# A hybrid encoder trunk in float32: where waiting work stands in VectorE's and ScalarE's order, how early the output projections load, and where the residual's factor goes

## The chip, the cores and the metric

The kernel runs on one core of a Trainium2 chip. The metric is the device time of one execution in microseconds (us), from the first to the last instruction with what lies around it; lower is better. The times shown are the median of three runs. The trace is one further execution that the hardware profiler recorded.

## The reference, cut to what matters

Two layers over a sequence of 2048 tokens of width 1024, in float32. Layer 0 mixes windowed attention with a gated short convolution, layer 1 mixes multi-head latent attention (8 heads, full 2048 x 2048 scores) with chunked spatial gating. Both end alike:

```python
def odd_mixer(x, pos, w_in, ...):
    cq, ckv, kr, du, dv, z = _split(x @ w_in, ODD_SIZES)
    ...
    yc = mla_attention(q_nope, q_rope, k_nope, k_rope, v)       # softmax(q k^T * scale) v, per head
    yd = chunked_spatial_gate(jax.nn.gelu(du), jax.nn.gelu(dv), v_ln_g, v_ln_b, w_s, b_s)
    y = jnp.concatenate([rms_norm(yc, c_norm), rms_norm(yd, d_norm)], axis=-1) * jax.nn.silu(z)
    return y @ w_out

# per layer i:
    h = layer_norm(DEEPNORM_ALPHA * x + y, post_ln_g[i], post_ln_b[i])      # ALPHA = 4 ** 0.25
    x = h + jax.nn.sigmoid(h @ ple_gate[i]) * (p[i] @ ple_proj[i])
```

Every matrix product is done to nearly full float32 accuracy: an operand is split into a rounded high part (`ScalarE` copy) and the low rest (a subtraction on `VectorE` or `GpSimd`), and a product takes three matmuls (high x high, high x low, low x high).

## The kernel before

There are four stages: `phase_a` (input projection of layer 0 with its mixers), `phase_out(0)` (its output projection and what follows it), `phase_c` (input projection of layer 1, spatial gating, latents, queries and keys), and `phase_d` (latent attention), which at its end starts `phase_out(1)`.

**Order of the work.** The program is traced in Python; a planner then chooses each engine's order from its own simulated times, and may move an instruction ahead of others on its engine when it thinks that the inputs are there. Each engine, and SP, which issues nearly all DMAs, then works strictly in that order. In `phase_d` TensorE alone keeps the order as traced. `tc.issue_after(ins)` (used by the change) makes what a block traces on the engine of `ins` stand behind `ins` in that engine's order.

**Attention (`phase_d`).** 8 heads x 4 query chunks of 512 are 32 blocks; a block goes over 16 key tiles (`kb`) of 128. Per key tile: three score matmuls (L1246 to 1248), the exponential on ScalarE in place in PSUM (L1249), the split into `ph` (ScalarE) and `pl` (VectorE, both L66/67 by way of L1252), the addition of `ph` into `acc` on GpSimd (L1257, L1259), one matmul for the row maxima of the block after next and its reduction on VectorE (L1136, L1137), and the two value matmuls (L1186, L1187) four key tiles later (`LAG`). `ph` has 7 buffers, `pl` 6, the scores 4 PSUM tiles. While block b runs, block b-1 is finished: at `kb` 3 its outputs leave for DRAM, at `kb` 7 its `acc` is split, at `kb` 9 `reciprocals` sums it over partitions with two matmuls, writes that row to DRAM, reads it back as 128 x 4 together with the sums of the low parts, adds (L1218), takes the reciprocal (L1219) and writes `rec` to DRAM. At the start of blocks 6, 9, ..., 27 one weight tile of the next stage is loaded and split (`out_weight`, L524). Operands of head h+1 are loaded in the blocks around its first use, through SP.

**Output projection (`phase_out`).** 16 token blocks of 128 tokens. `load(t)` (L572) loads the residual into `ox` and scales it by the square root of 2 on ScalarE (L576), and loads the operand tiles `ou` (three buffers, two per token block). In layer 1 the attention half of `ou` is made here from the three parts of the attention output: added on GpSimd (L594), times the broadcast `rec` (L595), squared for the RMS norm (L596), times the gate, split; `yc` and `szt` have one buffer, `ycm` and `rec` come from a ring of three raw tiles that the weight loads and the gate's input `praw` share. `first(t)` (L607) does the projection (48 matmuls), the scaled addition to the residual (L618) and the layer norm; `second(t)` (L628) transposes, multiplies by the two gate matrices (60 matmuls), and writes the result. The loop runs `first(t + 1)`, then `second(t)`. For layer 1, `next(self.output)` in the last attention block (L1269) loads the last two weight tiles and token block 0.

Of the kernel before, what the change touches and what calls it, by code (L numbers as in the profile page):

```python
# [31 lines left out]
SUM_AT = 9  # L32
START_AT = 2
# [19 lines left out]
class Builder:  # L53
# [467 lines left out]
    def out_weights(self, rings, src, ks, after=None):  # L521
        return list(self.out_weight(rings, src, ks, after))

    def out_weight(self, rings, src, ks, after=None):  # L524


        for k in ks:
# [6 lines left out]
            self.dma(raw, src[k * P:(k + 1) * P])  # L534
            eng = self.nc.gpsimd if k % 2 and src.shape[0] == D else self.nc.vector
# [18 lines left out]
    def phase_out(self, layer, es=None, wo=None, w_out=None, w_pr=None, right=None):  # L554


        tc, nc, I, c, d = self.tc, self.nc, self.i, self.c, self.d
# [9 lines left out]
        if right:  # L567
            w_out = w_out + self.out_weights(wo, I["w_out"][layer], range(len(w_out), 8))
            lng, lnb = self.out_norm(of, layer)
        xs, us = {}, {}  # L570

        def load(t):  # L572
            ts = slice(t * P, (t + 1) * P)
            x = xs[t] = xr.tile([P, D], F32, name="ox")
            self.dma(x, xin[ts])
            nc.scalar.activation(x, x, AF.Copy, scale=math.sqrt(2.0))  # L576
            us[t] = []
            for h in range(2):
                u = of.tile([P, 2, 4, P], F32R, name="ou", tag="ou", bufs=3)
                us[t].append(u)  # L580
                if layer == 1 and h == 0:
                    yc = of.tile([P, 4, P], F32, name="yc", tag="yc", bufs=1)
                    self.dma(yc, d["yc"][0, :, :, ts])
                    more = self.rr.tile([P, 2, 4, P], F32, name="ycm")
                    for a in range(2):
                        self.dma(more[:, a], d["yc"][1 + a, :, :, ts])
                    rec = self.rr.tile([P, 4, P], F32, name="rec")
                    for a in range(2):
                        self.dma(rec[64 * a:64 * a + 64],
                                 d["rec"].rearrange("(k a) s -> a k s", a=2)[a][:, ts].partition_broadcast(64))  # L590
                    sz = of.tile([P, 4, P], F32, name="szt", tag="szt", bufs=1)
                    self.dma(sz, d["szc"][:, :, ts])
                    for a in range(2):
                        nc.gpsimd.tensor_tensor(yc, yc, more[:, a], ALU.add)  # L594
                    nc.vector.tensor_tensor(yc, yc, rec, ALU.mult)  # L595
                    nc.scalar.activation(rec, yc, AF.Square)  # L596
                    nc.vector.tensor_tensor(sz, yc, sz, ALU.mult)
                    nc.gpsimd.tensor_tensor(rec[:, 0:2], rec[:, 0:2], rec[:, 2:4], ALU.add)
                    nc.gpsimd.tensor_tensor(rec[:, 0], rec[:, 0], rec[:, 1], ALU.add)
                    self.colsum(ss[:, 0, t:t + 1], rec[:, 0], self.psC("cs"))  # L600
                    self.rms(rs, ss, 0, slice(t, t + 1))
                    self.split(u[:, 0], u[:, 1], sz)
                    continue
                for a in range(2):
                    self.dma(u[:, a], d[ud][:, a, 4 * h:4 * h + 4, ts])

        def first(t):  # L607
            if t not in xs:
                load(t)
# [81 lines left out]
        for t in range(NB):  # L691
            if t + 1 < NB:
                first(t + 1)
            second(t)
# [688 lines left out]
```

## Time and profile before

| | us |
|---|---|
| median of three runs | 2961.62 (2958.94 to 2961.75) |
| the profiled execution's own time | 2963.46 |
| its span, first to last instruction | 2961.7 |
| TensorE busy | 2848.6 (96%) |
| VectorE busy | 1980.3 (67%) |
| ScalarE busy | 1351.7 (46%) |
| GpSimd busy | 1091.9 (37%) |

By the first and last instructions of each stage's lines, `phase_a` takes the first 720 us, `phase_out(0)` the next 430, `phase_c` up to 1683, attention from 1682.7 to 2493.8, `phase_out(1)` the rest. In the profile PE is TensorE, DVE VectorE, ACT ScalarE, POOL GpSimd, SP the queue that issues DMAs. A busy TensorE may still run at half its clock. A number in square brackets behind an instruction is the time its engine stood idle before it, with what ended that.

### The profile page before, as it was taken

Reading aid. Unit: us, or ns where it says so; the run is one execution under the profiler, and the core shown is the slowest. Engines: PE = TensorE matmul, PEld = TensorE weight load, DVE = VectorE, ACT = ScalarE, POOL = GpSimd, SP = SyncE. Lnnn points to the kernel's source line nnn. Section 1 sums busy time; section 2 is a strip of 40 time slices with the busy share of each in tenths; the row PEclk is TensorE's granted clock in tenths of the full one; section 3 lists DMA queues with packets and bytes.
Section 4 is the critical chain, followed back from the end, with each engine's and each line's share of the span. In section 5 each row is a group of like instructions: output and inputs, shape, how many; then the busy total and the mean of one; then the engine's idle time right before and its main releaser. Section 6 shows DMA issues by size and latency. Waiting matters only on the chain.

```text
span 2961.7 us, 38334 instructions
## 1 busy us (share of the span) xinstructions
PE 2848.6 (96%) x12808; PEld 2311.6 (78%) x12808; DVE 1980.3 (67%) x3956; ACT 1351.7 (46%) x2507; POOL 1091.9 (37%) x832
## 2 busy tenths in 40 slices
PE   8999999999999999999999999999999997799999
PEld 7888888888788888888888777777677765677787
DVE  3788467886644455446756788888888875456665
ACT  3554345454211123233432488888788875111111
POOL 0011001112411110120103187888888887423331
PEclk9999999999999999999999999999999998899999
DMA  7654465445444447216773403331333133333341
GB/s 227 181 144 138 142 192 161 131 125 191 137 119 132 127 132 265 85 62 231 247 236 93 114 17 81 81 81 25 81 84 70 48 81 90 101 106 114 106 116 43
DMA packets 316599, 365.27 MB, mean 123 GB/s; under 512 B 33248, under 2 KB 244368, under 8 KB 311280
## 3 DMA queue, kind: packets, MB, share of 16 engines
q1 hardware_dynamic: 288752, 333.38, 38.9%
q10 hardware_dynamic: 27648, 29.43, 2.8%
q8 instruction: 101, 1.65, 0.2%
q14 instruction: 98, 0.80, 0.1%
HBM read 238.19 MB, written 124.53 MB: 122 GB/s over the span
## 4 chain that ended last, share of the span: by engine, by line
PE 78%; DMA 9%; DVE 6%; ACT 2%; POOL 2%; issue 2%; SPq 1%; ACTq 0%; DVEq 0%; POOLq 0%
PE pg L88 6%; PE pa L77 6%; PE pa L76 6%; PE pa L78 6%; PE pm L1136 3%; PE pst L1246 3%; PE px L1186 3%; PE pst L1247 3%; PE py L1187 3%; PE pst L1248 3%; DMA rec<-rec 3%; PE pg L90 3%; PE py L76 3%; PE py L77 3%; PE pc L78 3%; PE py L78 3%
## 5 line engine op out<-in xcount | busy, mean ns | idle before, releaser
L1259 POOL TENSOR_TENSOR acc<-acc,ph 128x512 f32<-128x512 f32 x448 | 577.8, 1290 | 79.1 <-ACT ph L66 49.7
L67 DVE TENSOR_TENSOR pl<-pst,ph 128x512 fp32r<-128x512 f32 x512 | 347.0, 685 | 51.0 <-ACT ph L66 42.1
L1137 DVE TENSOR_REDUCE mx<-pm 128x1 f32<-128x512 f32 x512 | 348.9, 683 | 45.7 <-PE pm L1136 40.9
L1249 ACT ACTIVATE pst<-pst 128x512 f32<-128x512 f32 x512 | 296.1, 584 | 95.2 <-PE pst L1248 60.2
L76 PE MATMUL pa<-xh,w 128*128 128x512 f32 x832 | 328.5, 395 | 6.2 <-ACT xh L66 6.2
L77 PE MATMUL pa<-xl,w 128*128 128x512 f32 x832 | 328.9, 395 | 0.0
L78 PE MATMUL pa<-xh,w 128*128 128x512 f32 x832 | 328.0, 394 | 0.0
L66 ACT ACTIVATE ph<-pst 128x512 fp32r<-128x512 f32 x512 | 300.7, 597 | 30.1 <-POOL acc L1259 0.8
L625 POOL TENSOR_TENSOR ox<-ox,ln_g 128x1024 f32<-128x1024 f32 x32 | 77.1, 2409 | 485.1 <-DVE ox L624 462.1
L1136 PE MATMUL pm<-mkh,mqh 96*128 96x512 f32 x512 | 208.4, 407 | 29.6 <-DVE mx L1137 28.8
L76 PE MATMUL py<-wh,ou 128*128 128x512 f32 x512 | 210.0, 410 | 27.1 <-DVE ox L618 25.4
L1246 PE MATMUL pst<-mqh,mkh 97*128 97x512 f32 x512 | 209.7, 410 | 9.9 <-DVE pl L67 9.9
L1186 PE MATMUL px<-ph,mv 128*128 128x512 f32 x512 | 211.3, 413 | 2.9 <-ACT ph L66 2.9
L1247 PE MATMUL pst<-mql,mkh 96*128 96x512 f32 x512 | 208.0, 406 | 0.0
L88 PE MATMUL pg<-wh,oht 128*128 128x512 f32 x512 | 201.6, 394 | 6.1 <-DVE osg L650 5.3
L1187 PE MATMUL py<-pl,mv 128*66 128x512 f32 x512 | 207.1, 405 | 0.3 <-DVE pl L67 0.2
L77 PE MATMUL py<-wl,ou 128*128 128x512 f32 x512 | 206.8, 404 | 0.0
L1248 PE MATMUL pst<-mqh,mkl 96*128 96x512 f32 x512 | 206.3, 403 | 0.0
L78 PE MATMUL py<-wh,ou 128*128 128x512 f32 x512 | 204.8, 400 | 0.0
L88 PE MATMUL pg<-wl,oht 128*128 128x512 f32 x512 | 200.1, 391 | 0.0
L76 PEld LDWEIGHTS pa<-xh,w 128*128 128x128 f32 x832 | 157.2, 189 | 37.6 <-ACT xh L66 6.9
L77 PEld LDWEIGHTS pa<-xl,w 128*128 128x128 f32 x832 | 157.1, 189 | 31.3 <-DVE xl L67 1.2
(377 smaller groups left out, 6200.0 us busy)
## 6 DMA issues: line engine op xcount, KB each, us to landing
ou<-u SPq DMA_DIRECT2D x96, 256.0 KB
qw<-q SPq DMA_DIRECT2D x64, 256.0 KB
x1T<-oxt SPq DMA_DIRECT2D x64, 256.0 KB
cx<-x1T SPq DMA_DIRECT2D x16, 1024.0 KB
q<-st SPq DMA_DIRECT2D x32, 256.0 KB
u<-ua SPq DMA_DIRECT2D x32, 256.0 KB
wraw<-in_w_out SPq DMA_DIRECT2D x16, 512.0 KB
ox<-in_x SPq DMA_DIRECT2D x16, 512.0 KB
```

The lines of the kernel that those rows point to most:

```text
L66: self.nc.scalar.activation(hi, src, AF.Copy)
L67: (eng or self.nc.vector).tensor_tensor(lo, src, hi.bitcast(F32), ALU.subtract)
L76: mm(ps, ah, bh, start=start, stop=False)
L77: mm(ps, ah, bl, start=False, stop=False)
L78: mm(ps, al, bh, start=False, stop=stop)
L88: mm(ps, a[:, 0, k], b[k][part][:, cols], start=k == 0 and part == 0, stop=False)
L1136: nc.tensor.matmul(ps, qh[0:96, q0:q0 + P], kh[0:96, kc * CH:(kc + 1) * CH], start=True, stop=True)
L1137: nc.vector.tensor_reduce(self.mx[blk][:, b, kc:kc + 1], ps, AX.X, ALU.max)
L1186: mm(x, v[:, kb, 0:P], ph, start=kb == 0, stop=kb == 15)
L1246: mm(ps, kh[0:97, ks], qh[0:97, qs], start=True, stop=False)
L1247: mm(ps, kh[0:96, ks], ql[0:96, qs], start=False, stop=False)
L1259: nc.gpsimd.tensor_tensor(acc, acc, pf, ALU.add)
```

## The change

Three things. In attention, the split of a weight tile and VectorE's two operations on the row sums are taken apart from the loads that they wait for, and stand behind the work of key tiles 13 and 15 in ScalarE's and VectorE's order; the last sums are split on VectorE. In the output projection `load` becomes `fetch`, `fetch_x` (loads) and `prep` (work): `fetch(t + 3)` is traced after `first(t + 1)`, `prep(t + 2)` stands behind the last scaled addition of `first(t + 1)` on VectorE, and in layer 1 `first(0)` comes right behind attention's last value matmuls, before the last sums are totalled. The residual is no longer scaled: the projection's factor is divided by the square root of 2 in `rms` instead, and the layer norm's epsilon is halved.

```diff
+WEIGHT_AT = 13
...
     def out_weight(self, rings, src, ks, after=None):
...
             self.dma(raw, src[k * P:(k + 1) * P])
+            yield None
             eng = self.nc.gpsimd if k % 2 and src.shape[0] == D else self.nc.vector
             self.split(h[:, k % 2], l[:, k % 2], raw, eng)
...
     def rms(self, rs, ss, half, b):
-        self.rsqrt(self.cp, rs[:, half, b], ss[:, half, b], 4.0 / 512, 4 * EPS, b.stop - b.start)
+        self.rsqrt(self.cp, rs[:, half, b], ss[:, half, b], 8.0 / 512, 8 * EPS, b.stop - b.start)
...
-        def load(t):
...
-            nc.scalar.activation(x, x, AF.Copy, scale=math.sqrt(2.0))
...
+        def fetch(t):
+            ts = slice(t * P, (t + 1) * P)
+            us[t] = [None, None]
+            if layer == 1:
+                yc = of.tile([P, 4, P], F32, name="yc", tag="yc", bufs=1)
+                self.dma(yc, d["yc"][0, :, :, ts])
+                more = self.rr.tile([P, 2, 4, P], F32, name="ycm")
...
+                att[t] = yc, more, rec, sz
+            for h in range(layer, 2):
+                u = us[t][h] = of.tile([P, 2, 4, P], F32R, name=f"ou{h}", tag="ou", bufs=OU)
                 for a in range(2):
                     self.dma(u[:, a], d[ud][:, a, 4 * h:4 * h + 4, ts])
 
+        def fetch_x(t):
+            x = xs[t] = xr.tile([P, D], F32, name="ox")
+            self.dma(x, xin[t * P:(t + 1) * P])
+
+        def prep(t):
+            if layer == 0:
+                return
+            yc, more, rec, sz = att.pop(t)
+            u = us[t][0] = of.tile([P, 2, 4, P], F32R, name="ou0", tag="ou", bufs=OU)
+            for a in range(2):
+                nc.gpsimd.tensor_tensor(yc, yc, more[:, a], ALU.add)
+            nc.vector.tensor_tensor(rec, yc, rec, ALU.mult)
+            sq = more[:, 0]
+            nc.scalar.activation(sq, rec, AF.Square)
+            nc.vector.tensor_tensor(sz, rec, sz, ALU.mult)
...
+            self.split(u[:, 0], u[:, 1], sz)
+            self.colsum(ss[:, 0, t:t + 1], sq[:, 0], self.psC("cs"))
+            self.rms(rs, ss, 0, slice(t, t + 1))
...
         if right:
-            load(0)
+            fetch(0)
+            fetch_x(0)
+            w_out = w_out + self.out_weights(wo, I["w_out"][layer], range(len(w_out), 8))
+            lng, lnb = self.out_norm(of, layer)
+            prep(0)
+            yield
+            first(0)
             yield
...
-        first(0)
-        load(1)
+            prep(0)
+            first(0)
+        fetch(1)
+        fetch_x(1)
+        prep(1)
         w_pr = w_pr or self.out_weights(wp, I["ple_proj"][layer], range(2))
         w_g = self.out_weights(wg, I["ple_gate"][layer], range(8))
+        fetch(2)
+        fetch_x(2)
+        if right:
+            self.mla_rest()
         for t in range(NB):
             if t + 1 < NB:
                 first(t + 1)
+            if t + 2 < NB:
+                with tc.issue_after(last[0].ins):
+                    prep(t + 2)
+            if t + 3 < NB:
+                fetch(t + 3)
             second(t)
+            if t + 3 < NB:
+                fetch_x(t + 3)
...
-        def reciprocals(h, qc, hl):
+        def total(h, qc, hl):
             ps = self.psC("psum")
...
             self.dma(rec, d["sums"][h, :, qs].rearrange("a (p j) -> p a j", j=4))
+            return rec
+
+        def reciprocals(h, qc, rec):
             nc.vector.tensor_tensor(rec[:, 0], rec[:, 0], rec[:, 1], ALU.add)
             nc.vector.reciprocal(rec[:, 0], rec[:, 0])
             self.dma(d["rec"][h, qs].rearrange("(p j) -> p j", j=4), rec[:, 0])
...
-                if blk in range(6, 28, 3):
+                loads = blk in range(6, 28, 3)
+                if loads:
                     after.append(old[4])
-                    weights.append(next(steps))
+                    next(steps)
...
-                        nc.scalar.activation(ps, ps, AF.Exp, scale=scale)
+                        ex = nc.scalar.activation(ps, ps, AF.Exp, scale=scale)
...
-                        self.split(ph, pl, ps)
+                        nc.scalar.activation(ph, ps, AF.Copy)
                         pf = ph.bitcast(F32)
+                        behind = nc.vector.tensor_tensor(pl, ps, pf, ALU.subtract)
...
                             if kb == SUM_AT:
-                                reciprocals(*old[:2], hl)
+                                rec = total(*old[:2], hl)
+                            if kb == 15:
+                                with tc.issue_after(behind.ins):
+                                    reciprocals(*old[:2], rec)
+                        if loads and kb == WEIGHT_AT:
+                            with tc.issue_after(ex.ins), tc.issue_after(behind.ins):
+                                weights.append(next(steps))
                 old = (h, qc, x, y, acc)
-        while queue:
-            values()
-        finish(*old[:4])
-        reciprocals(*old[:2], sums(old[4]))
+            while queue:
+                values()
+            finish(*old[:4])
+            hl = sums(old[4], nc.vector)
+            self.c_bufs = 3
+            self.ps_open("pse")
+            next(self.output)
+            rec = total(*old[:2], hl)
         es.close()
-        self.c_bufs = 3
-        self.ps_open("pse")
+        self.mla_rest = lambda: reciprocals(*old[:2], rec)
```

## Rows read from the trace of the kernel before

**Rows 1.** The page's second part: TensorE's busy tenths in 40 slices.

```profile
PE   8999999999999999999999999999999997799999
```

**Rows 2.** Windows: busy us (x instructions) of each engine, clock, DMA share, GB/s.

```profile
721.00:801.00 80.00, 74.30 (x313) 59.83 (x314) 59.66 (x124) 19.79 (x26) 27.63 (x11) 0.94 0.59 189
...
1709.40:2426.40 717.00, 686.91 (x2872) 522.65 (x2872) 610.56 (x1021) 593.73 (x1085) 606.52 (x476) 0.97 0.28 65
...
1709.40:1732.40 23.00, 23.00 (x100) 17.71 (x100) 20.57 (x36) 20.29 (x38) 20.52 (x17) 1.00 0.09 19
...
1778.60:1807.80 29.20, 25.09 (x100) 18.74 (x99) 21.95 (x38) 20.67 (x39) 21.08 (x17) 0.92 0.71 158
...
1804.00:1809.00 5.00, 5.00 (x12) 3.73 (x13) 4.29 (x8) 1.18 (x2) 0.79 (x1) 0.50 0.03 5
...
1977.00:2008.70 31.70, 26.02 (x101) 19.57 (x100) 22.17 (x37) 20.76 (x39) 21.34 (x19) 0.89 0.68 163
...
2277.60:2309.10 31.50, 26.00 (x100) 19.52 (x99) 22.12 (x37) 20.80 (x39) 21.36 (x19) 0.89 0.74 180
...
2426.40:2462.50 36.10, 26.14 (x85) 18.50 (x84) 19.01 (x27) 21.61 (x42) 26.98 (x24) 0.76 0.28 77
...
2462.50:2493.80 31.30, 24.96 (x93) 16.76 (x91) 20.42 (x34) 24.06 (x44) 24.83 (x19) 0.92 0.29 87
...
2493.80:2611.50 117.70, 89.18 (x347) 70.61 (x348) 49.52 (x136) 19.61 (x30) 45.95 (x30) 0.83 0.39 103
...
2611.50:2961.70 350.20, 340.43 (x1543) 277.99 (x1541) 207.62 (x539) 61.24 (x100) 106.36 (x64) 1.00 0.33 97
```

**Rows 3.** Waits in block 4: total us, times, longest.

```profile
DVE rec L1218 <- DMA rec<-sums: 5.2, 1, 5.2
...
PE pm L1136 <- DVE mx L1137: 4.1, 1, 4.1
```

**Rows 4.** SP's timeline in block 4: start, us, issue.

```profile
1788.55 7.69 SPq L72 DMA_DIRECT2D yc<-oa  x2
...
1800.23 0.39 SPq L72 DMA_DIRECT2D rec<-sums  x1
```

**Rows 5.** ScalarE's timeline in block 12: start, us, instruction, idle before it.

```profile
1995.09 1.06 ACT L66 ACTIVATE wh<-wraw 128x1024 fp32r<-128x1024 f32 x1 [6.08 <-DMA wraw<-in_w_out]
```

**Rows 6.** VectorE's timeline in blocks 1 and 4.

```profile
1727.82 0.16 DVE L1218 TENSOR_TENSOR rec<-rec 128x4 f32<-128x4 f32 x1 [0.31 <-DMA rec<-sums]
...
1733.22 0.69 DVE L67 TENSOR_TENSOR pl<-pst,ph 128x512 fp32r<-128x512 f32 x1
...
1802.06 0.52 DVE L1218 TENSOR_TENSOR rec<-rec 128x4 f32<-128x4 f32 x1 [5.24 <-DMA rec<-sums]
```

**Rows 7.** Waits in blocks 30 and 31.

```profile
PE pst L1246 <- DVE pl L67: 7.6, 2, 4.5
...
DVE yc L595 <- issue: 5.7, 1, 5.7
```

**Rows 8.** The page's costliest groups: GpSimd's additions.

```profile
L1259 POOL TENSOR_TENSOR acc<-acc,ph 128x512 f32<-128x512 f32 x448 | 577.8, 1290 | 79.1 <-ACT ph L66 49.7
```

**Rows 9.** VectorE's timeline: one operation of the inverse root, twice.

```profile
2468.85 1.14 DVE L104 SCALAR_TENSOR_TENSOR rs<-rsq,rs 128x1 f32<-128x1 f32 x1
...
2544.86 0.16 DVE L104 SCALAR_TENSOR_TENSOR ost<-rsq,ost 128x1 f32<-128x1 f32 x1
```

**Rows 10.** Waits from 2493.8 to 2611.5.

```profile
DVE yc L595 <- DMA rec<-rec: 25.4, 3, 11.5
...
PE py L76 <- DVE ox L618: 20.6, 4, 7.5
...
ACT ox L576 <- DMA ox<-x: 15.3, 1, 15.3
```

**Rows 11.** SP's timeline: the broadcast of reciprocals for token block 2.

```profile
2515.39 1.28 SPq L72 DMA_DIRECT2D rec<-rec  x2
```

**Rows 12.** Waits of the whole span: ScalarE's split of the gate input.

```profile
ACT opt L66 <- PE pp L90: 80.3, 19, 6.4
```

More of the change, by code (lines that the diff above doesn't have):

```diff
@@ L517, in colsum, with out_weights @@
         self.nc.vector.tensor_copy(out, ps.rearrange("p (b m) -> p b m", m=P)[:, 0:n, 0])
-    def out_weights(self, rings, src, ks, after=None):
-        return list(self.out_weight(rings, src, ks, after))
+    def out_weights(self, rings, src, ks):
+        return [w for w in self.out_weight(rings, src, ks) if w]
     def out_weight(self, rings, src, ks, after=None):
@@ L566, in phase_out @@
         xr = Ring(es, tc, f"ox{layer}", 1 if right else 3, right)
[L567 to L570, printed above, removed]
-        def load(t):
-            ts = slice(t * P, (t + 1) * P)
-            x = xs[t] = xr.tile([P, D], F32, name="ox")
-            self.dma(x, xin[ts])
-            nc.scalar.activation(x, x, AF.Copy, scale=math.sqrt(2.0))
[L577 to L603, printed above, removed]
@@ new lines, in phase_out @@
+        xs, us, att, last = {}, {}, {}, {}
+        OU = 3
+        def fetch(t):
+            ts = slice(t * P, (t + 1) * P)
+            us[t] = [None, None]
[4 more added lines that the diff above has]
+                for a in range(2):
+                    self.dma(more[:, a], d["yc"][1 + a, :, :, ts])
+                rec = self.rr.tile([P, 4, P], F32, name="rec")
+                for a in range(2):
+                    self.dma(rec[64 * a:64 * a + 64],
+                             d["rec"].rearrange("(k a) s -> a k s", a=2)[a][:, ts].partition_broadcast(64))
+                sz = of.tile([P, 4, P], F32, name="szt", tag="szt", bufs=1)
+                self.dma(sz, d["szc"][:, :, ts])
+                att[t] = yc, more, rec, sz
+            for h in range(layer, 2):
+                u = us[t][h] = of.tile([P, 2, 4, P], F32R, name=f"ou{h}", tag="ou", bufs=OU)
@@ L604, in load @@
                 for a in range(2):
                     self.dma(u[:, a], d[ud][:, a, 4 * h:4 * h + 4, ts])
+        def fetch_x(t):
[6 more added lines that the diff above has]
+            u = us[t][0] = of.tile([P, 2, 4, P], F32R, name="ou0", tag="ou", bufs=OU)
+            for a in range(2):
+                nc.gpsimd.tensor_tensor(yc, yc, more[:, a], ALU.add)
[3 more added lines that the diff above has]
+            nc.vector.tensor_tensor(sz, rec, sz, ALU.mult)
+            nc.gpsimd.tensor_tensor(sq[:, 0:2], sq[:, 0:2], sq[:, 2:4], ALU.add)
+            nc.gpsimd.tensor_tensor(sq[:, 0], sq[:, 0], sq[:, 1], ALU.add)
+            self.split(u[:, 0], u[:, 1], sz)
+            self.colsum(ss[:, 0, t:t + 1], sq[:, 0], self.psC("cs"))
+            self.rms(rs, ss, 0, slice(t, t + 1))
@@ L607, in first @@
         def first(t):
-            if t not in xs:
-                load(t)
             x, u = xs[t], us.pop(t)
@@ L617, in first @@
                         self.mm3(ps, u[h][:, 0, k], u[h][:, 1, k], wh[:, ns], wl[:, ns], k == 0, k == 3)
-                    nc.vector.scalar_tensor_tensor(x[:, ns], ps, rs[:, h, t:t + 1], x[:, ns], ALU.mult, ALU.add)
+                    last[0] = nc.vector.scalar_tensor_tensor(x[:, ns], ps, rs[:, h, t:t + 1], x[:, ns],
+                                                             ALU.mult, ALU.add)
             st = self.cp.tile([P, 20], F32, name="ost", tag="ost", bufs=3)
@@ L679, in phase_out @@
         if not right:
-            load(0)
+            fetch(0)
+            fetch_x(0)
             w_out = w_out + self.out_weights(wo, I["w_out"][layer], range(len(w_out), 8))
@@ L1201, in finish, with sums @@
             self.dma(d["sums"][h, 1:2, qs], oy[64:65])
-        def sums(acc):
+        def sums(acc, eng):
             hl = sp.tile([P, 2, CH], F32R, name="acs", tag="acs", bufs=1)
-            self.split(hl[:, 0], hl[:, 1], acc, nc.gpsimd)
+            self.split(hl[:, 0], hl[:, 1], acc, eng)
             return hl
-        def reciprocals(h, qc, hl):
+        def total(h, qc, hl):
             ps = self.psC("psum")
@@ L1215, in reciprocals @@
             self.dma(d["sums"][h, 0:1, qs], row)
-            rec = sp.tile([P, 2, 4], F32, name="rec", tag="rec", bufs=2)
+            rec = self.cp.tile([P, 2, 4], F32, name="rec", tag="rec", bufs=2)
             self.dma(rec, d["sums"][h, :, qs].rearrange("a (p j) -> p a j", j=4))
+            return rec
+        def reciprocals(h, qc, rec):
+            qs = slice(qc * CH, (qc + 1) * CH)
             nc.vector.tensor_tensor(rec[:, 0], rec[:, 0], rec[:, 1], ALU.add)
```

4 lines of the change are left out of this document (2 added, 2 removed).

## The prediction

> **What bounds the kernel now.** I read the busy tenths first: TensorE is at 9 in every slice but the first and a few near four fifths of the span [rows 1]. So TensorE is the bound almost everywhere, and only what keeps it waiting, or makes it slow, can be won. The windows then say where that is [rows 2]. An undisturbed attention block (32 of them, block b begins with the first score matmul of its 16 key tiles) takes 23.0 us with TensorE busy for all of it at clock 1.00. Blocks 1 to 29 take 717.0 us together, though 29 x 23.0 is 667.0: 50.0 us too much. Blocks 30 and 31 take 36.1 and 31.3 us although they have only some 85 to 93 matmuls. The next 117.7 us hold 347 matmuls, the 350.2 us after that 1543: at 350.2 / 1543 = 0.227 us the 347 would take 78.8 us, so 38.9 us are lost there. These three sums, 50, about 25 and 39 us, are what there is to win; the rest is at TensorE's own pace.
>
> The waits say who did it. In block 4 VectorE stood 5.2 us for the DMA that brings back the row sums, and TensorE then 4.1 us for VectorE's maximum, because a score-maximum tile was not read [rows 3]. SP's own timeline shows why that DMA is late in this block: an earlier issue (attention outputs, behind the next head's keys and values) took 7.69 us, and the read of the sums was issued only at 1800.23 [rows 4]. In block 12 it is ScalarE that stands, 6.08 us, for a weight DMA [rows 5]; VectorE's subtraction is behind it. After such a stall the granted clock falls: 0.50 in the 5 us from 1804 (the level of 1.2 GHz) against 1.00 in block 1 [rows 2]. So a wait of 4.1 us makes block 4 29.2 - 23.0 = 6.2 us longer.
>
> **The change, part by part.**
>
> *Reciprocals of the row sums.* Same instructions, but VectorE's add and reciprocal now stand behind the subtraction of key tile 15. In block 1 the add starts at 1727.82, the tile-15 subtraction at 1733.22 [rows 6]: 5.4 us, plus 0.6 for the subtraction itself, so the add comes at about block start + 24.4. In block 4 the wait ended at 1802.06, which is block start + 23.5 [rows 6]. The wait of 5.2 us therefore goes, with about 0.9 us in hand. The six blocks in which a new head's operands are loaded (4, 8, 12, 16, 20, 24; rows 2 show the first, the longest and the last) take 29.2, 29.1, 31.7, 30.4, 29.4 and 31.5 us, together 181.3: 43.3 us above six undisturbed ones; the other 6.7 us of the 50.0 lie in the blocks just after a stall and in block 28, where ScalarE waits for the residual's load. What is late next: the same add, in those of the six whose sums come later in the block than block 4's. Behind it on VectorE are the first subtraction and maximum of the next block, and four key tiles of scores are in flight before TensorE needs them; block 1's wait of 0.31 us cost nothing [rows 6]. The write of the reciprocals to DRAM moves along, past the load issues of the next block on SP; the output projection reads it more than a block later.
>
> *Weight steps (8 of them).* The load stays at the block's start, the ScalarE copy and the VectorE subtraction go behind key tile 13 (POOL's subtraction of the odd ones follows the copy). Same work; the wait of 6.1 us of block 12 (and of 24) goes, since the copy began at 1995.09 [rows 5], block start + 18.1, and tile 13 comes later: its subtraction at about + 21 (tile 15's at + 23.8 less two tiles of 23.0 / 16 us), its exponential somewhat before. Cost of the work itself: nothing on the path, it lies beside matmuls in blocks that have 2 to 3 us of ScalarE and VectorE idle time [rows 2].
>
> Together I take 44 of the 50 us (0.2 us left over in each of the 29 blocks). Bounds: 50 if no wait is left; near 0 if another transfer of the same six blocks ends just as late.
>
> *Blocks 30 and 31.* In these VectorE stands 5.7 us at the first token block's product with the reciprocals, and TensorE waits 7.6 us for subtractions [rows 7]. The preparation of token block 1 is now traced behind the end of attention, the last sums are split on VectorE instead of POOL, and the first projection fills TensorE while the last total is formed. But the preparation of token block 0 still has no place written out for it, and the reciprocals that it reads are written 6 us later, so its wait may stay. The nearest floor is POOL: 32 additions of 1.29 us [rows 8], 41.3 us, plus some 6 us for one split, two additions and a weight, 47 us against 67.4 now. I take 52 us, 15 saved; bounds 2 (the wait and the half clock stay) and 27 (TensorE's 165 matmuls at 23.0/99 = 0.232 us, 38.3 us, plus 2).
>
> The small operations of the inverse root bear on this. On a 128x1 tile one of them takes 1.14 us at 2468.85, while POOL adds, and 0.16 us at 2544.86, when POOL is idle [rows 9]. The Trainium skill, "SBUF — State Buffer", section "SBUF: two separate sides", has a rule for it: VectorE (with two SBUF inputs) and GpSimd take a shared pair of ports as an exclusive lock for a whole instruction, and the loser waits. The rows agree with it. By it the chain stays slow in block 31 of the new kernel too, since POOL adds without a break there, and the 15 would not become 27; by the 0.16 us row alone a further 5 us or so would go.
>
> *The first token blocks of the second output projection.* Of the 38.9 us lost, the waits name TensorE behind VectorE's scaled addition 20.6 us, VectorE behind the reciprocals' broadcast 25.4 us (longest 11.5), ScalarE behind the residual's load 15.3 us [rows 10]; the rest is the half clock, 0.83 on average [rows 2]. The broadcast for token block 2 is issued only at 2515.39 [rows 11], for it shares three raw buffers with the gate weights. After the change the residual has no ScalarE step, so 15.3 us of waiting go; token block t+2 is prepared behind the last scaled addition of t+1, and its loads were issued a block earlier. What stays: eight gate weights through three buffers before the first second half, and token block 2, whose loads are traced behind those weights while its preparation is pinned behind token block 1. I let 17 us stay and take 22; bounds 5 (each of the three long broadcast waits merely changes its token block) and 37.
>
> *Steady token blocks.* The 350.2 us hold the last 13 token blocks, less what went ahead; the idle time left there is 350.2 - 340.4 = 9.8 us [rows 2]. I take 4; bounds -5 and 9. *First projection (layer 0).* Its preparation is empty, the scaling on ScalarE goes, and only three operand tiles exist as before, so its loads get no further ahead: 80.0 us with 5.7 us idle [rows 2], of which I take 1; bounds -5 and 5. *No scaling of the residual:* the factor goes into two constants that exist already; 32 ScalarE passes go, on an engine that is far from full in that stage (61.2 us of 350.2 [rows 2]). Nothing beyond what is counted above.
>
> Sum: 44 + 15 + 22 + 4 + 1 = 86 us. The profiled execution took 2963.5 us (span 2961.7); 2963.5 - 86 = 2877.5. The runs' median is 1.8 us below that execution: 2876.
>
> **Rivals.**
> *A, only attention gains.* Token blocks 0 to 3 wait for broadcasts and gate weights as before, since both still go through three raw buffers and one accumulator tile. For it: the preparation of token block 0 is not pinned, and its input is written later. Against it: the longest waits there are VectorE's, and pinning puts other work of VectorE ahead of them. 44 + 1 saved: 2917.
> *B, the six blocks keep half their loss.* The reserve of 0.9 us is small and was worked out in one of the six blocks; another late transfer (the row of maxima, also queued behind the 7.69 us issue) could stop TensorE at the next block's start. 22 instead of 44 saved: 2898.
> *C, slower: SP is blocked in every token block.* Loads for t+3 are traced ahead of the second half of t. They need the single accumulator tile that the preparation of t+2 frees only after the last scaled addition of t+1. If they stand before the gate input's load in SP's order, that load waits for the preparation: 0.7 us for the product, eight issues of 0.64 us (two take 1.28 [rows 11]), 1.8 us to land (the sums' read, issued at 1800.23 [rows 4], ended VectorE's wait at 1802.06 [rows 6]) and two splits of at most 0.69 us [rows 6], 9 us in all, less 8 transposes at 0.227 us that TensorE has to do meanwhile: 7 us idle in each of 13 token blocks, 91 us, and some 3 us each at half clock, as in block 4, 39 us. Less 60 us won in attention that is +70: 3032. It decides from 60 / 13 = 4.6 us of added time per token block. For it: SP is in order, and rows 4 show one issue holding the next ones for 7.69 us. Against it: ScalarE's split of the gate input waited 80.3 us for its buffer to be free, which shows that its load is early now [rows 12], and each token block has 350.2 / 13 = 27 us to keep it so. The Trainium skill, "DMA: Bandwidth & Descriptors", section "Anatomy of one DMA — SWDGE (gpsimd) path", says that a DMA's semaphore wait is spent on the issuing sequencer; rows 4 agree, and this is what would make C dear.
> *D, no difference:* the waits only change their names, 2962.
>
> **Chances.** Forecast 0.66, A 0.16, B 0.08, C 0.06, D 0.04. About 0.2% (6 us) is what a measurement of this kernel can tell from no change. The forecast's own range is 2842 to 2900, with each term about halfway to its bounds. With A and B it becomes 2842 to 2925, which leaves out C, D and the best corner of the forecast. Faster 0.90, within 0.2% 0.04, slower 0.06.
>
> **What would show it.** Blocks 4, 8, ..., 24 at 23 to 24 us with clock 1.00, and no long wait of VectorE for the sums, show the first two steps right; 27 us or more shows B. Blocks 30 and 31 at 50 to 55 us together show the third; a product with the reciprocals that still waits 5 us there says that its wait moved with its input. In the 120 us after attention, TensorE's wait for the scaled addition should fall from 20.6 us to below 10. C would show as TensorE waiting for the split of the gate input in each token block. The prediction is wrong if the attention blocks stay above 700 us for 1 to 29, or if the token blocks of either layer grow above 26.5 us each.

## The result: 2916.9 us, and the profile after

The median after the change is 2916.89 us (2914.39 to 2919.84) against 2961.68 before: ratio 0.9851 [0.9834, 0.9868], 44.8 us faster. The forecast was 86 us. The profiled execution took 2919.13 us, 44.3 less than the one before, and its stages say where those came from. Each stage is cut at the same events as before, but for the end of attention, which is cut some 0.6 us early here and in the later runs. First the windows of the kernel after: blocks 1 to 29; block 4; blocks 30 and 31; from there to token block 4 of the second output projection; the rest; and 5 us in that rest.

```profile
1707.70:2387.80 680.10, 671.25 (x2872) 511.07 (x2871) 618.66 (x1020) 595.55 (x1083) 609.06 (x476) 1.00 0.30 67
1777.60:1801.10 23.50, 23.09 (x100) 17.62 (x99) 21.35 (x36) 20.37 (x38) 20.57 (x17) 1.00 0.90 197
2387.80:2413.10 25.30, 22.67 (x85) 16.37 (x84) 15.08 (x25) 19.95 (x40) 20.52 (x18) 0.87 0.40 101
2413.10:2451.00 37.90, 27.97 (x92) 19.40 (x90) 22.39 (x36) 24.10 (x43) 31.74 (x25) 0.77 0.27 75
2451.00:2543.90 92.90, 81.23 (x337) 65.54 (x338) 62.81 (x151) 17.80 (x27) 38.69 (x23) 0.93 0.42 117
2543.90:2917.30 373.40, 348.86 (x1553) 284.60 (x1552) 202.13 (x529) 51.66 (x92) 111.26 (x70) 0.98 0.34 96
2657.00:2662.00 5.00, 3.93 (x15) 3.61 (x16) 3.92 (x17) 1.82 (x3) 0.94 (x2) 0.66 0.54 175
```

Against the rows of before [rows 2]:

| stage | before | after | saved | forecast |
|---|---|---|---|---|
| up to block 1 (layer 0 is in it) | 1709.4 | 1707.7 | 1.7 | 1 |
| attention blocks 1 to 29 | 717.0 | 680.1 | 36.9 | 44 |
| blocks 30 and 31 | 67.4 | 63.2 | 4.2 | 15 |
| first token blocks, second output projection | 117.7 | 92.9 | 24.8 | 22 |
| the remaining token blocks | 350.2 | 373.4 | -23.2 | 4 |

The attention gain is there and so is the gain at the start of the projection; the second is given back almost whole in the token blocks that follow. (Some 10 matmuls, about 2 us of work, moved from the fourth line to the fifth.)

The waits of TensorE in that last stage name the cause:

```profile
PE cs L517 <- POOL ycm L612: 12.2, 5, 3.8
PE py L77 <- ACT ou L67: 5.9, 3, 2.0
PE py L77 <- DVE ox L626: 0.8, 1, 0.8
PE pg L89 <- ACT oht L67: 0.3, 1, 0.3
```

None of these lines existed before; there the list of TensorE's waits held only these two:

```profile
PE pg L88 <- DVE osg L650: 3.9, 8, 1.2
PE py L76 <- DVE osg L650: 0.8, 1, 0.8
```

TensorE's idle time in the stage grew from 350.2 - 340.4 = 9.8 us to 373.4 - 348.9 = 24.5. The other 8.4 us of the loss are busy time: the 10 matmuls that moved, and a clock of 0.98 instead of 1.00. `cs` is the column sum of squares (TensorE, with a matrix of ones), the only matmul in a token block's preparation; `ou` is the operand tile that the same preparation makes. One of the five stalls in the timeline, rows of four engines picked out in order of time:

```profile
2654.29 0.75 DVE L626 SCALAR_TENSOR_TENSOR ox<-py,rs,ox 128x512 f32<-128x512 f32 x1
...
2654.96 0.68 DVE L607 TENSOR_TENSOR rec<-yc,rec 128x512 f32<-128x512 f32 x1
...
2655.73 0.63 ACT L609 ACTIVATE ycm<-rec 128x512 f32<-128x512 f32 x1 [2.21 <-DVE rec L607]
...
2656.43 0.72 POOL L611 TENSOR_TENSOR ycm<-ycm 128x256 f32<-128x256 f32 x1 [15.60 <-ACT ycm L609]
...
2657.24 0.78 POOL L612 TENSOR_TENSOR ycm<-ycm 128x128 f32<-128x128 f32 x1
...
2658.07 0.80 PE L517 MATMUL cs<-ones,ycm 128*128 128x128 f32 x2 [2.46 <-POOL ycm L612]
```

The first row is the scaled addition behind which the preparation is pinned. From it the chain runs VectorE, ScalarE, GpSimd, GpSimd, TensorE: 3.8 us. GpSimd stood 15.6 us for the squares, since the pin lets the chain begin no earlier, and TensorE has the column sum next in its order, ahead of the transposes of the second half. It stands 2.46 us, and the granted clock of the 5 us around it is 0.66 (part of it at 1.2 GHz). The same wait stands once among the first token blocks too, 5.3 us long. The nine token blocks 4 to 12 take 28.1 us each on average, 26.6 before: (2796.7 - 2543.9) / 9 and (2851.1 - 2611.5) / 9, from the first matmul of each.

Not every token block stalls. The column sums of blocks 5, 8, 11 and 14 wait, and behind them that of block 15. In these TensorE does no projection matmul of the same block first; in the two blocks between, it does 16 or 6 of them ahead of the column sum, which then comes without a wait, as in block 6:

```profile
2607.38 0.38 PE L517 MATMUL cs<-ones,ycm 128*128 128x128 f32 x2
```

Why the planner orders them so was not looked into.

In blocks 30 and 31 two waits are left. The first is that of the product with the reciprocals, 5.7 us before [rows 7]; the second is TensorE's, behind a chain of VectorE's 128x1 operations. Timelines of VectorE, GpSimd and TensorE after the change:

```profile
2396.77 0.69 DVE L607 TENSOR_TENSOR rec<-yc,rec 128x512 f32<-128x512 f32 x1 [3.72 <-DMA rec<-rec]
...
2423.27 2.34 POOL L68 TENSOR_TENSOR wl<-wraw,wh 128x1024 fp32r<-128x1024 f32 x1 [0.36 <-ACT wh L67]
...
2423.35 2.27 DVE L104 SCALAR_TENSOR_TENSOR rsq<-rsq 128x1 f32<-128x1 f32 x1
...
2426.28 0.80 PE L1281 MATMUL pst<-mqh,mkh 97*128 97x512 f32 x1 [5.78 <-DVE pl L1289]
```

The 128x1 operation, 0.16 us elsewhere [rows 9], begins 0.08 us after GpSimd's and ends 0.01 us after it.

Last, the small loss in blocks 1 to 29: TensorE's only large wait in them.

```profile
PE pmt L1176 <- DVE mx L1167: 8.1, 19, 0.6
```

Most blocks take 23.4 to 23.6 us where 23.0 had been usual. The pinned reciprocals stand ahead of the last maxima on VectorE, and the transpose of the maxima waits 0.4 us.

### The profile page after: what moved, and what is told of

The parts are those of the page before. It is cut to its first block, busy times and chain, and to the rows that moved or that the text cites. A ratio compares the mean times of both kernels' runs of the same rounds, so it can differ in the third digit from the quotient of the medians.

```text
span 2917.3 us, 38322 instructions
## 1 busy us (share of the span) xinstructions
PE 2830.8 (97%) x12808; PEld 2300.1 (79%) x12808; DVE 1993.4 (68%) x3957; ACT 1323.9 (45%) x2475; POOL 1092.1 (37%) x831
## 4 chain that ended last, share of the span: by engine, by line
PE 83%; DVE 6%; DMA 6%; ACT 2%; issue 2%; SPq 1%; POOL 1%; ACTq 0%; DVEq 0%; POOLq 0%
PE pg L89 7%; PE pa L78 6%; PE pa L79 6%; PE pa L77 6%; PE pg L91 4%; PE py L77 4%; PE pst L1281 4%; PE pst L1282 3%; PE py L78 3%; PE pst L1283 3%; PE pm L1166 3%; PE px L1216 3%; PE py L79 3%; PE py L1217 3%; PE pc L79 3%; PE pc L78 3%
## 5 line engine op out<-in xcount | busy, mean ns | idle before, releaser
L658 ACT ACTIVATE osg<-pg 128x512 f32<-128x512 f32 x64 | 38.3, 598 | 374.7 <-PE pg L91 369.7
```

## The experiments

Times are medians; ratios are against runs of the kernel before on the same chip. Two theories were at stake for the lost 23 us: that the pin (with the column sum in it) makes TensorE wait, or that something else in the new order of loads and buffers does.

**1. attn_only: the attention part alone** (before, with the reciprocals and weight steps pinned; projections and scaling as before).

```diff
...
+                            if kb == 15:
+                                with tc.issue_after(behind.ins):
+                                    reciprocals(*old[:2], rec)
+                        if loads and kb == WEIGHT_AT:
+                            with tc.issue_after(ex.ins), tc.issue_after(behind.ins):
+                                weights.append(next(steps))
...
```

> The kernel before with the attention part of the change alone (weight splits behind key tile 13, reciprocals behind key tile 15; the output projections, the scaling and the end of attention as before). Theory 1, attention made nearly all of the gain: blocks 1 to 29 take about 680 us as in the changed kernel (717 before), the rest as before, 2925 us (2920 to 2930). Rival, the gain needs the new output projection too: the blocks still take over 700 us, 2945 us or more.

Measured 2925.03 us, ratio 0.9881 [0.9862, 0.9901]. Blocks 1 to 29 and block 28 alone:

```profile
1709.40:2396.70 687.30, 674.29 (x2873) 512.96 (x2872) 621.60 (x1021) 597.10 (x1085) 611.29 (x476) 1.00 0.30 67
...
2341.80:2373.20 31.40, 26.66 (x100) 19.27 (x99) 26.01 (x38) 22.79 (x41) 25.32 (x19) 0.89 0.31 76
```

29.7 of the 36.9 us come with the pins alone. The other 7 are block 28, 31.4 us here and 24.45 after the whole change. TensorE waits twice in it:

```profile
PE pmt L1148 <- DVE mx L1139: 2.6, 1, 2.6
PE pm L1138 <- ACT srow L1216: 2.2, 1, 2.2
```

The first wait is for maxima that stand behind a weight split of 2.80 us on VectorE, the second is behind ScalarE, which stands 2.7 us for the residual's load. The kernel after has 0.6 us of the first kind there and none of the second. By the medians attn_only is 37.9 us faster than before, so some 8 us of its gain lie behind block 29; the expected time came out although blocks 1 to 29 missed the 680 us expected of them.

**2. out_only: the rest alone** (after, with the attention pins undone).

```diff
                     next(steps)
+                    weights.append(next(steps))
...
-                            if kb == 15:
-                                with tc.issue_after(behind.ins):
-                                    reciprocals(*old[:2], rec)
-                        if loads and kb == WEIGHT_AT:
-                            with tc.issue_after(ex.ins), tc.issue_after(behind.ins):
-                                weights.append(next(steps))
+                                reciprocals(*old[:2], rec)
```

> The changed kernel with the attention part taken back (weights split at the start of their block, reciprocals traced right behind the totals, neither pinned); output projections, residual and the end of attention as changed. Theory 1, the output projection gives back in its steady token blocks what it wins at its start: blocks 1 to 29 near 717 us again, second output projection near 466 us, 2953 us (2946 to 2960). Rival, the output projection is a gain that attention's part spoils: 2940 us or less.

Measured 2970.76 us, ratio 1.0024 [1.0012, 1.0036]: the output part by itself makes the kernel slightly slower. A gain of some 10 us had been expected, so the direction was missed. Its last twelve token blocks (366.3 us) show the same waits as the whole change:

```profile
PE cs L517 <- POOL ycm L612: 11.4, 4, 3.8
PE py L77 <- ACT ou L67: 7.9, 4, 2.0
```

**3. late_sum: the column sum traced later** (on after). Token block t+2's preparation stays pinned, but its column sum and inverse root are traced behind the second half of t; the squares get a tile of their own.

```diff
-            nc.gpsimd.tensor_tensor(sq[:, 0], sq[:, 0], sq[:, 1], ALU.add)
+            s = squares[t] = of.tile([P, P], F32, name="sqs", tag="sqs", bufs=1)
+            nc.gpsimd.tensor_tensor(s, sq[:, 0], sq[:, 1], ALU.add)
...
             second(t)
+            if t + 2 < NB:
+                norm(t + 2)
...
```

> The changed kernel, but in the loop the sum of squares over partitions (a TensorE matmul) and the inverse root of token block t+2 are traced behind the second half of t instead of with its preparation; the squares get a tile of their own, and a table of positions moves to another pool to make room. Theory 1, TensorE waits for that matmul because it stands in its order right behind the first half while its input goes through VectorE, ScalarE and GpSimd in turn: the waits of about 2.45 us and the half clock after them go, 2899 us (2893 to 2907). Rival, the preparation as a whole is too late behind the last scaled addition (operand tile, loads): TensorE then waits as long for the operand tile, 2912 us or more.

Measured 2881.70 us, ratio 0.9728 [0.9711, 0.9745]: 35 us less than after, twice the expected gain. The same stage has no wait of TensorE left, clock 1.00, and token blocks of 25.64 us:

```profile
2546.30:2881.10 334.80, 329.42 (x1513) 272.98 (x1511) 206.62 (x523) 49.20 (x89) 108.64 (x70) 1.00 0.36 104
```

Per matmul that is 334.8 / 1513 = 0.221 us, against 0.240 after and 0.227 before. The squares' own tile also sets a raw buffer free a step earlier; the next run has no such tile.

**4. no_pin: the pin taken away** (after, preparation traced at the same place, not pinned).

```diff
-                with tc.issue_after(last[0].ins):
-                    prep(t + 2)
+                prep(t + 2)
```

> The changed kernel without the pin: the preparation of token block t+2 is traced behind the first half of t+1, but its VectorE work is free to go ahead of the last scaled addition. Theory 1, the place of the sum of squares in TensorE's order is what costs, not the pin: TensorE still waits for it or for the operand tile, 2910 to 2935 us. Rival, the pin makes the chain so late: without it the waits go, 2885 to 2900 us.

Measured 2890.47 us, ratio 0.9758 [0.9743, 0.9772]. The theory that wanted 2910 us or more without the pin fell: taking the pin away gains 26 us on the kernel after.

```profile
2545.30:2888.70 343.40, 339.30 (x1545) 279.88 (x1543) 229.94 (x541) 50.69 (x91) 114.90 (x70) 1.00 0.37 103
```

TensorE has no wait in this stage either. For token block 5 the chain's first product and its column sum, VectorE's row, then TensorE's:

```profile
2553.21 2.86 DVE L607 TENSOR_TENSOR rec<-yc,rec 128x512 f32<-128x512 f32 x1 [2.94 <-POOL yc L606]
...
2570.20 0.38 PE L517 MATMUL cs<-ones,ycm 128*128 128x128 f32 x2
```

The product starts 17.0 us ahead of the column sum; in the kernel after, the two were 3.1 us apart (2570.67 and 2573.78) and TensorE stood 2.45 us for it. So it takes both, a pin that starts the chain late and a TensorE step at its end that stands next in TensorE's order. Either one undone removes the waits. The planner made a new order in both runs. No_pin's token blocks still take 26.1 us against late_sum's 25.64; why was not traced.

**5. late_prep0: the first token block's norm later** (late_sum, with the column sum and inverse root of token block 0 behind the end of attention).

```diff
             prep(0)
-            norm(0)
             yield
+            norm(0)
             first(0)
```

> As late_sum, but for token block 0 the sum of squares over partitions and the inverse root are traced behind the end of attention too (right before its first half), not in the last attention block. Theory 1, the inverse root's small VectorE operations, slowed by GpSimd's additions to 1.1 to 2.3 us each, hold the subtractions of the last block for some 9 us, and TensorE waits 5 us for them and runs at half clock afterwards: the last attention block takes 30 to 33 us instead of 39, 2874 us (2870 to 2877) against 2882. Rival, the last block is held by GpSimd's additions and the weight splits, and the wait only moves: 2879 us or more.

Measured 2875.94 us, ratio 0.9708 [0.9694, 0.9723]. Block 31 takes 31.6 us where late_sum had 39.2, and the inverse root's operations, now after GpSimd's additions, take 0.16 us each.

```profile
2412.20:2443.80 31.60, 24.65 (x90) 16.42 (x89) 15.08 (x22) 23.57 (x42) 30.68 (x25) 0.95 0.22 71
...
2451.71 0.16 DVE L104 SCALAR_TENSOR_TENSOR rsq<-rsq 128x1 f32<-128x1 f32 x1
```

**6. load_next: loads traced later** (late_prep0, with the loads of t+2 traced ahead of the first half of t+1, behind the second half of t-1 instead of ahead of it).

```diff
-        fetch(2)
         fetch_x(2)
...
         for t in range(NB):
+            if t + 2 < NB:
+                fetch(t + 2)
             if t + 1 < NB:
                 first(t + 1)
...
-            if t + 3 < NB:
-                fetch(t + 3)
             second(t)
```

> late_prep0 with the loads of a token block traced one block later (ahead of the first half of t+1 instead of the second half of t-1), all else the same. Theory 1 (the loads were not what bound the second output projection; the order of the dependent steps was): within 6 us of late_prep0's 2876, token blocks 25.6 to 26 us each, no new wait of the product with the reciprocals above 1 us that reaches TensorE. Rival (the loads ahead are what keeps the broadcast out of the path): the product waits about 5 us per block and TensorE 2 to 3 us with half clock behind it, 13 blocks: 2910 us or more.

Measured 2872.18 us, ratio 0.9691 [0.9675, 0.9707], with the stage at 334.4 us:

```profile
2540.10:2874.50 334.40, 329.11 (x1513) 272.86 (x1511) 205.91 (x523) 48.95 (x89) 108.83 (x70) 1.00 0.37 104
```

The time and the token blocks are as the first theory said, but they do not decide between the two, since the loads did not move. SP's issue of a load of `yc`, in late_prep0, then here:

```profile
2612.14 0.52 SPq L73 DMA_DIRECT2D yc<-yc  x1
...
2610.62 0.53 SPq L73 DMA_DIRECT2D yc<-yc  x1
```

The next token block's first matmul comes at 2618.5 and 2617.0: 6.4 us behind the issue in both. `yc` has one buffer, which the product of the token block ahead sets free. What an earlier or later load would be worth here stays open.

**7. max3: the maxima one tile later** (after, with the row of maxima finished one key tile later).

```diff
-MAX_AT = 2
+MAX_AT = 3
```

> The changed kernel with the maxima of the next block taken at key tile 3 instead of 2. Theory 1, the reciprocals behind key tile 15 delay VectorE's reduction of the maxima at the next block's start, and TensorE waits 0.4 us for it in most blocks, which then take 23.5 instead of 23.0 us: blocks 23.0 to 23.1 us, 29 x 0.4 = 12 us less, 2906 us (2902 to 2910). Rival, VectorE is simply 0.4 us behind there, and the next instruction that needs it waits instead: no change, 2914 to 2920 us.

Measured 2918.27 us, ratio 0.9853 [0.9836, 0.9869]: no change, as the rival said. TensorE waits the same total, in 16 pieces instead of 19:

```profile
PE pmt L1176 <- DVE mx L1167: 8.1, 16, 1.1
```

**8. recip_next: reciprocals half a block later** (late_sum; behind key tile 6 of the next block instead of tile 15).

```diff
                             if kb == SUM_AT:
                                 rec = total(*old[:2], hl)
-                            if kb == 15:
+                                done.append((*old[:2], rec))
+                            if kb == REC_AT and len(done) == 1:
                                 with tc.issue_after(behind.ins):
-                                    reciprocals(*old[:2], rec)
+                                    reciprocals(*done.pop())
...
```

> As late_sum, but VectorE's two operations on the row sums stand behind key tile 6 of the next block instead of behind key tile 15. Theory 1, at key tile 15 they fall on the stretch where VectorE has no time in hand (its maxima are due two key tiles later), in the middle of a block they cost nothing, as they did at key tile 10 before: blocks 23.0 us, 0.4 us less in most of them, 2871 us (2867 to 2876) against 2882. Rival, the 0.4 us is VectorE's total work in a block and stays wherever they stand: 2878 us or more.

Measured 2878.13 us, ratio 0.9715 [0.97, 0.9729]. The 0.4 us per block do go: blocks 1 to 29 take 671.4 us, 9 less than in late_sum. But block 31 takes 49.0:

```profile
1706.90:2378.30 671.40, 668.70 (x2873) 513.04 (x2872) 611.83 (x1020) 594.31 (x1083) 608.86 (x476) 1.00 0.29 67
2400.30:2449.30 49.00, 32.79 (x91) 22.03 (x91) 29.16 (x40) 26.08 (x47) 34.56 (x28) 0.69 0.36 111
```

Its timelines show what filled it, first GpSimd's, then VectorE's, then TensorE's:

```profile
2410.32 2.81 POOL L69 TENSOR_TENSOR wl<-wraw,wh 128x1024 fp32r<-128x1024 f32 x1
...
2410.84 2.31 DVE L104 TENSOR_TENSOR rsq<-rs 128x1 f32<-128x1 f32 x1
2413.18 0.65 DVE L105 SCALAR_TENSOR_TENSOR rsq<-rsq 128x1 f32<-128x1 f32 x1
2413.87 1.18 DVE L106 SCALAR_TENSOR_TENSOR rs<-rsq,rs 128x1 f32<-128x1 f32 x1
...
2421.18 0.80 PE L1292 MATMUL pst<-mqh,mkh 97*128 97x512 f32 x1 [9.68 <-DVE pl L1300]
```

VectorE spends 2410.84 to 2420.5 on nine such operations, and the subtraction that TensorE needs is behind them. So the time is the rival's (2878 us or more), but not for its reason, and its interval overlaps that of late_sum.

**9. best: late_prep0 and recip_next together.** The diffs are those of both.

> The kernel with the reciprocals of the row sums pinned behind key tile 6 of the next block, and both the sum of squares traced late and that of token block 0 behind the end of attention. Theory 1 (the loss of recip_next in block 31, 49 us instead of 39, is TensorE held by the sum of squares of token block 0): with that matmul behind attention the gain of blocks 1 to 29 (680 to 671 us) and of block 30 (25 to 22) is kept: about 2864 us, block 31 at 32 to 34 us, blocks 1 to 29 at 671. Rival (the last block is long because the reciprocals themselves now reach DRAM later, and the product of token block 0 with them): block 31 stays above 40 us and the time at 2874 or above.

Measured 2871.26 us, ratio 0.9691 [0.9676, 0.9705], 46 us less than the kernel after. Blocks 1 to 29 keep their 671.4 us; the 9.68 us stall is gone, block 31 takes 37.5 instead of 49.0:

```profile
2401.90:2439.40 37.50, 31.56 (x89) 21.44 (x89) 21.13 (x27) 25.29 (x46) 34.86 (x28) 0.69 0.40 121
```

That is between the two theories: the later inverse root takes 11.5 us off block 31, but token block 0's product with the reciprocals still falls in it, and the clock stays at 0.69, against 0.95 in late_prep0. That the product is what keeps it there is not shown, and moving it too was not tried. The interval overlaps that of late_prep0.

**10. scale_only: no scaling alone** (before, with the residual's scaling removed and the constants changed, nothing else).

```diff
-            nc.scalar.activation(x, x, AF.Copy, scale=math.sqrt(2.0))
...
-        self.rsqrt(self.cp, rs[:, half, b], ss[:, half, b], 4.0 / 512, 4 * EPS, b.stop - b.start)
+        self.rsqrt(self.cp, rs[:, half, b], ss[:, half, b], 8.0 / 512, 8 * EPS, b.stop - b.start)
...
```

> The kernel before with the residual left unscaled and nothing else changed (the factor in the inverse root of the projection and in the layer norm's epsilon). Theory 1, ScalarE's wait for the residual's load, 15.3 us at the start of the second output projection, delays VectorE's scaled addition and TensorE, and this goes: 2955 us (2950 to 2959). Rival, VectorE then waits for the same load itself: no change, 2960 us or more.

Measured 2946.54 us, ratio 0.9943 [0.9927, 0.996]: 14 us by the medians, 17 by the ratio, more than expected. Token blocks 0 to 3, before and here, from the first matmul of block 0 to that of block 4, then the rest here:

```profile
2501.60:2611.50 109.90, 87.82 (x346) 69.82 (x345) 48.58 (x136) 16.15 (x26) 39.85 (x26) 0.86 0.38 99
...
2499.10:2599.90 100.80, 85.91 (x345) 68.94 (x344) 52.41 (x147) 12.98 (x22) 37.60 (x23) 0.87 0.38 102
2599.90:2944.50 344.60, 338.44 (x1545) 279.04 (x1543) 206.41 (x528) 49.62 (x91) 107.68 (x68) 1.00 0.34 100
```

The first four give 9.1 us, which is what the first theory expected, only more: TensorE's wait for the scaled addition falls there from 20.6 to 12.0 us. The rest gives 350.2 - 344.6 = 5.6 us; most steady token blocks take 25.8 us instead of 26.3 to 27.3.

**11. scale_back: the scaling put back** (late_prep0 with the 32 ScalarE passes and the old constants).

```diff
+            nc.scalar.activation(x, x, AF.Copy, scale=math.sqrt(2.0))
...
-        self.rsqrt(self.cp, rs[:, half, b], ss[:, half, b], 8.0 / 512, 8 * EPS, b.stop - b.start)
+        self.rsqrt(self.cp, rs[:, half, b], ss[:, half, b], 4.0 / 512, 4 * EPS, b.stop - b.start)
...
```

> late_prep0 with the residual scaled by ScalarE again (32 passes) and the constants as before. Theory 1 (removing the scaling was worth something by itself, as scale_only's 14 us say): about 2886 to 2890 us, the token blocks of the second output projection near 26.3 us instead of 25.6. Rival (the gain of scale_only came from the load and its ScalarE step standing at the head of a token block's work, which the new order has moved away in any case): no difference, 2876 within 4 us.

Measured 2880.35 us, ratio 0.9719 [0.9704, 0.9733], against 0.9708 [0.9694, 0.9723] without: the intervals overlap. The median lies between the two theories' times, nearer the rival's 2876. The token blocks do not differ from late_prep0's (334.6 us):

```profile
2541.40:2876.50 335.10, 329.43 (x1513) 272.90 (x1511) 204.61 (x523) 59.59 (x100) 108.84 (x70) 1.00 0.37 104
```

So ScalarE's 10 us of scaling in that stage cost nothing by themselves. By that, what scale_only gained came from the old place of the load and its scaling, at the head of each token block's own chain; the new order takes them away from there in any case. Whether a few microseconds remain elsewhere is open.

## Why 86 us were forecast and 44.8 came

*Attention, 44 forecast, 36.9 measured.* The six blocks went from 29.1 to 31.7 us down to 23.2 to 23.5, as worked out, and rival B (half the loss kept) did not come. I allowed 0.2 us left over per block; 680.1 - 667.0 = 13.1 us is 0.45 per block. I had named what is queued behind the moved addition ("the first subtraction and maximum of the next block") and excused it by four key tiles of scores in flight. The maxima were not covered by that: their transpose follows early in the block, and the nineteen waits sum to 8.1 us. recip_next shows it by taking most of them away (2.1 us in five waits are left).

*Blocks 30 and 31, 15 forecast, 4.2 measured.* The bounds 2 to 27 held; the value was too hopeful. The product's wait moved with its input, 5.7 to 3.7 us, which the prediction had named. The chain of the inverse root stayed slow in block 31: 2.27 us beside GpSimd's 2.34, and 5.78 us of TensorE's time behind it. That is what the prediction took from the rule on the shared ports in the Trainium skill ("SBUF — State Buffer", "SBUF: two separate sides"), and the trace agrees with it. I used it only to cap the gain and did not ask what else is queued on VectorE behind nine such operations. late_prep0 puts their price in block 31 at 7.6 us by its profile; the net gain, 5.8 us by the medians, lies where the intervals of its ratio and late_sum's overlap.

*First token blocks, 22 forecast, 24.8 measured.* Right in size; about 2 of it is work that moved. TensorE's wait for the scaled addition fell from 20.6 us [rows 10] to 4.3. The causes are less certain than the size: from the first matmul of block 0 to that of block 4 it is 109.9 us before, 101.2 in attn_only, 100.8 in scale_only, 95.4 in out_only and 92.3 after. Each part alone gains some of it, the attention part too, which the prediction had not counted here, and the gains do not add up.

*Steady token blocks, "I take 4; bounds -5 and 9": -23.2 measured.* This is the step that failed. The prediction counted the preparation's VectorE, ScalarE and DMA work and never that it ends in a TensorE matmul. Pinned behind the last scaled addition of t+1, the chain of 3.8 us starts when TensorE has little left ahead of that matmul. Rival C saw the same shape, TensorE held by a chain that starts with the preparation, but put it on SP's queue and at 10 us per block; SP was not the cause, since late_sum cures it with the loads left alone. The sign of being wrong that I set ("above 26.5 us each") was met in this layer, at 28.1; but it was set badly, since the blocks took 26.6 before.

*No scaling, "Nothing beyond what is counted above".* scale_only gives 14 to 17 us for it alone, scale_back nothing that can be told from zero on top of the new order. Its 9.1 us in the first token blocks fall where the prediction had counted ScalarE's wait in its 22; its 5.6 us in the steady ones were not counted.

*Rival A (2917, only attention gains)* gives the measured time, but not by its own mechanism: the first token blocks did gain 24.8 us, and the token blocks behind them lost 23.2. The measured time lies outside the forecast's own range, 2842 to 2900, and inside the wider one, up to 2925, only because a loss that was not forecast ends near that rival's sum. That is luck.

*Sums.* The forecast's own range does not follow from its terms: each halfway to its bounds gives 2855 to 2921, which would have held the measured time. In the bounds of blocks 30 and 31, the rows hold 85 + 93 = 178 matmuls, not 165, so at most 24 us could be saved, not 27. Rival C's 3 us of half clock "as in block 4" are 6.2 - 4.1 = 2.1 us there. None of this bears on the step that failed.

With the one failing step mended (late_sum) and the norm of token block 0 moved (late_prep0) the kernel takes 2875.94 us, close to the forecast's 2876. That the sum is met is in part luck too: by its stages late_prep0 saves 2 us up to block 1, 37 in blocks 1 to 29, 11 in blocks 30 and 31, 20 in the first token blocks and 16 in the rest (some 7 of these are matmuls done a stage earlier), where 1, 44, 15, 22 and 4 were forecast. best and load_next, at 2871 and 2872 us, beat both kernels by the most; between the two there is no difference.

## What to carry to other kernels

When a step is pinned behind an instruction, follow its chain to the last engine that it touches: if it ends on the engine that sets the time, the pin puts that engine behind the whole chain's latency unless enough other work stands ahead in its order, and either the end of the chain must be traced later or the pin dropped. Ask the same of each small operation that is moved: not what it costs alone, but what stands behind it on its engine while a neighbour slows it. A change of several parts should be timed part by part, since here one part alone was a loss that the sum hid.

## What the runs showed of the hardware

The small operations were not just slower beside GpSimd, but ended with GpSimd's instruction: 2.27 us beside a 2.34 us split after the change, 2.31 us (2410.84 to 2413.15) beside one that ran from 2410.32 to 2413.13 in recip_next, where 0.16 us is their own time. Beside a longer GpSimd instruction, one 128x1024 split instead of a 128x512 addition of 1.3 us, the same 128x1 operation on VectorE took about twice as long (2.27 against 1.22 us in the kernel after).
